# A decoder trunk on one core: the scan norm's squares in a tile of their own, three weight splits behind the last layer norm of a stage, and the small operations of the final norm first

## The chip, the cores and the metric

The kernel runs on one core of a Trainium2 chip. A core has a matrix engine (TensorE, "PE" in the profile, with its weight loads shown apart as "PEld"), a vector engine (VectorE, "DVE"), a scalar engine (ScalarE, "ACT"), GpSimd ("POOL") and SyncE ("SP"), which here issues the transfers between DRAM and the on-chip memory. Each engine works through its own instructions in a fixed order and waits on semaphores for what the others make. The metric is the device time of one execution in microseconds. Before the change three runs took 1351.21, 1352.62 and 1352.86 us, so the median is 1352.62 us.

## The reference

The reference is a two-layer decoder trunk on a residual stream of 512 tokens by 1024 columns, in float32:

1. A Mamba-2 (SSD) mixer: an input projection, a causal depthwise convolution of width 4 with SiLU, a chunked scan over 8 groups of 4 heads, a gate, a root-mean-square norm inside each group, and an output projection.
2. `h = layer_norm(alpha * h + mix)`.
3. A gated feed-forward network (FFN) with a causal depthwise convolution of width 3: `(silu(g) * val) @ down`, hidden size 2816, and again `h = layer_norm(alpha * h + ff)`.
4. A latent-attention layer (8 heads) with a layer norm, and a second FFN with the final layer norm, whose result is the output.

The group norm of step 1 is the place of the first part of the change:

```
yg = y.reshape(b, s, G, SSD_D_INNER // G)
yg = yg * lax.rsqrt(jnp.mean(yg * yg, axis=-1, keepdims=True) + LN_EPS)
```

## The kernel before, in words

**Products.** Every float32 product is made of three passes on TensorE. A weight tile is split into a rounded part `wh` (a cast on ScalarE, line 60) and a rest `wl` (a subtraction on VectorE, line 61); activations are split in the same way into index 0 and index 1 of a tile. `mm_a` (line 117, matmuls at line 124) adds `wh` times the rounded activations, `wl` times the rounded ones and `wh` times their rest; `mm_b` (lines 130 to 132) does the same with the operands' roles turned round.

**The weight stream.** `WStream` holds the list of all weight tiles of the four stages in the order of use. A tile is loaded by SP into one of 3 staging buffers (`wst`, line 47), then split into one of 6 pairs of `wh` and `wl`. `ahead(i, la)` splits up to item `i + la`, but never more than 6 beyond the last retired one; `get` calls it with the default of 4. A staging buffer comes free when line 61 has read it, so a late split makes a later load late; a pair comes free when TensorE has used it.

**Order.** Python emits the instructions, and a planner then orders those of PE, DVE, ACT and POOL with its own costs; SP's transfers keep the order in which the program emits them (a load is emitted when a split makes room in the staging buffers). A tile in a pool of one buffer gets its next writer only after the last reader of the old contents is done, and the planner puts that writer where it expects this to be.

**The scan.** For each group `g`, `chain(g)` has seven steps. Step s2 (line 551) multiplies the decay matrix W (line 560) and makes `xdt` (line 565) and `wx` (line 567) from transposed inputs in PSUM. Step s3 multiplies `wx` on TensorE (line 574), then W and `xdt` (line 585). Step s4 ends with the sum of squares `sq` (line 608), which lies in the buffer of `wx` (`tag="wx"`). Step s5 reads `sq` on TensorE (line 614), s6 makes the group's factor `rstd`. For groups 0 to 6 the program has s5 of the group before ahead of s2; for the last group, 7, s5 of group 6 comes after s2 of group 7, just ahead of s3. Output projections (`out_part`, lines 130 to 132, and the addition to `h` on VectorE, line 150) fill the time between.

**From the scan to the first FFN.** The last `out_part` of each of four token blocks is followed by `ln_apply`: a sum on DVE (line 157), the squares on ACT (line 159), the power -0.5 on POOL (lines 160 and 161), and the normalisation on DVE (lines 164 and 167). `transpose_h` then transposes the block on TensorE (line 208), and ACT and DVE split the transposes into `ht` (lines 211 and 212). The transposes of the last two blocks are kept in `k.pend`. The FFN starts with its first four weight tiles, here called n to n+3, on tokens 0 to 255, flushes `k.pend` ahead of the fourth, and then does the four again on tokens 256 to 511 (lines 276 to 281). The weights n to n+2 are split before; n+3 to n+5 are split as the FFN asks for them.

**The final norm.** `ln_last` (line 169) normalises the last token block in two pieces of columns as TensorE ends them: statistics of the first 768 columns (lines 181 to 185), then of the last 256 (lines 186 to 191), the power on POOL (line 192), and the two normalising operations over the columns with the output transfers (lines 194 to 198).

## Time and profile before

| what | value |
|---|---|
| median of three runs | 1352.62 us |
| the profiled execution, its own time | 1353.32 us |
| span of that execution in the profile | 1351.6 us |
| mean granted clock of TensorE over the span | 0.995 |
| busy share of PE, PEld, DVE, ACT, POOL | 99%, 83%, 65%, 43%, 5% |
| moved by the DMA engines | 135.14 MB, 100 GB/s on the mean |

Times inside the profile count from the start of the span. A row of the timeline gives start, length, engine, line and operation, with "xN" where several were merged; in square brackets stands how long the engine had been idle before it and what released it. A row of the windows view gives the length of a stretch, then the busy time of PE, PEld, DVE, ACT and POOL with their instruction counts in brackets, the TensorE clock that was granted on the mean (1.00 is full speed), the busy share of the DMA engines and GB/s. Matmuls are pipelined, so the distance of their starts tells more than their length.

### The profile page before, as it was taken

The page shows a single profiled execution, that of the slowest core. Times are in us where ns is not written, and L with a number is a line of the kernel's source. Part 1 is how long each engine was busy: PE and PEld are TensorE (multiplying, and loading weights), DVE is VectorE, ACT ScalarE, POOL GpSimd, SP SyncE. Part 2 cuts the span into 40 slices and gives each one's busy share as a digit, 9 for nine tenths or more (in the row PEclk, how much of TensorE's full clock was granted, in tenths as well). Part 3 has the DMA queues.
Part 4 walks back from the last instruction along what each step waited for, and adds up shares of the span by engine and source line. Part 5 has one row for each costly group of instructions (what it writes and reads, how often), then busy time and mean ns, then how long its engine had stood idle before and what let it go on. Part 6 is the DMA issues. An engine that isn't in the chain of part 4 may idle for free.

```text
span 1351.6 us, 17208 instructions
## 1 busy us (share of the span) xinstructions
PE 1335.6 (99%) x6827; PEld 1126.3 (83%) x6827; DVE 879.8 (65%) x1326; ACT 586.3 (43%) x934; POOL 70.8 (5%) x71
## 2 busy tenths in 40 slices
PE   9999999999999999999999999999999999999997
PEld 8888888888878888888888889888898888888886
DVE  7788888778788655525655366987576553465534
ACT  5765546545533444313443134665254432344421
POOL 0111001101102000000000021000100000000001
PEclk9999999999999999999999999999999999999999
DMA  7533332332322333232332222211052322323211
GB/s 241 185 101 122 110 119 69 110 125 79 109 94 64 142 99 103 87 102 94 102 101 86 86 89 65 86 54 64 32 190 94 98 98 89 106 95 103 91 55 63
DMA packets 44433, 135.14 MB, mean 100 GB/s; under 512 B 4768, under 2 KB 5792, under 8 KB 42816
## 3 DMA queue, kind: packets, MB, share of 16 engines
q1 hardware_dynamic: 44352, 134.04, 30.1%
q8 instruction: 53, 0.87, 0.3%
q14 instruction: 28, 0.23, 0.1%
HBM read 131.86 MB, written 2.16 MB: 99 GB/s over the span
## 4 chain that ended last, share of the span: by engine, by line
PE 90%; DVE 5%; issue 1%; DMA 1%; ACT 1%; POOL 1%; SPq 0%; POOLq 0%; DVEq 0%; ACTq 0%
PE ps L124 55%; PE ps L130 9%; PE ps L131 9%; PE ps L132 9%; PE ps L1039 2%; PE ps L585 1%; PE ps L1073 1%; PE ps L574 1%; DVE wl L61 1%; PE ps L593 1%; DVE h L150 1%; PE ps L1060 1%; PE ps L693 1%; PE ps L208 1%; PE ps L556 1%
## 5 line engine op out<-in xcount | busy, mean ns | idle before, releaser
L124 PE MATMUL ps<-ht,wh 128*128 128x512 f32 (+1 forms) x2272 | 519.5, 379 | 0.5 <-DVE ht L212 0.3
L124 PEld LDWEIGHTS ps<-ht,wh 128*128 128x128 f32 x2272 | 409.7, 189 | 79.7 <-issue 1.0
L61 DVE TENSOR_TENSOR wl<-wst,wh 128x1024 fp32r<-128x1024 f32 (+3 forms) x226 | 265.4, 1179 | 154.3 <-ACT wh L60 153.9
L60 ACT CAST wh<-wst 128x1024 fp32r<-128x1024 f32 (+3 forms) x226 | 228.1, 1014 | 229.0 <-PE ps L132 168.7
L124 PE MATMUL ps<-ht,wl 128*128 128x512 f32 (+1 forms) x1136 | 267.9, 378 | 0.0
L124 PEld LDWEIGHTS ps<-ht,wl 128*128 128x128 f32 x1136 | 206.5, 189 | 39.5
L130 PE MATMUL ps<-wh,gt 128*128 128x512 f32 (+1 forms) x363 | 139.1, 383 | 0.0
L132 PE MATMUL ps<-wh,gt 128*128 128x512 f32 (+1 forms) x363 | 138.9, 383 | 0.0
L131 PE MATMUL ps<-wl,gt 128*128 128x512 f32 (+1 forms) x363 | 138.9, 383 | 0.0
L243 DVE SCALAR_TENSOR_TENSOR acc<-ps,cw,acc 128x511 f32<-128x511 f32 x88 | 65.5, 746 | 97.1 <-ACT acc L242 97.1
L446 DVE SCALAR_TENSOR_TENSOR cv<-ps,cw,cv 128x511 f32<-128x511 f32 (+2 forms) x96 | 71.4, 745 | 37.9 <-ACT cv L444 37.2
L242 ACT ACTIVATE acc<-ps,cw 128x512 f32<-128x512 f32 x88 | 68.5, 779 | 40.3 <-PE ps L124 40.3
L132 PEld LDWEIGHTS ps<-wh,gt 128*128 128x128 f32 x363 | 68.2, 188 | 13.3
L131 PEld LDWEIGHTS ps<-wl,gt 128*128 128x128 f32 x363 | 68.2, 188 | 13.3
L130 PEld LDWEIGHTS ps<-wh,gt 128*128 128x128 f32 x363 | 68.2, 188 | 13.2
L249 ACT CAST gt<-acc 128x512 fp32r<-128x512 f32 x44 | 27.3, 621 | 98.6 <-DVE acc L248 98.6
L244 DVE SCALAR_TENSOR_TENSOR acc<-ps,cw,acc 128x510 f32<-128x510 f32 x88 | 65.6, 748 | 2.8
L150 DVE SCALAR_TENSOR_TENSOR h<-h,ps 128x512 f32<-128x512 f32 x47 | 31.2, 683 | 55.0 <-PE ps L132 55.0
L247 ACT ACTIVATE acc<-acc 128x512 f32<-128x512 f32 x44 | 27.8, 632 | 86.9 <-DVE acc L244 86.9
L160 POOL TENSOR_SCALAR lnst<-lnst 128x1 f32<-128x1 f32 x15 | 11.6, 772 | 867.9 <-ACT lnjunk L159 867.9
L548 ACT ACTIVATE W<-W,cum 128x128 f32<-128x128 f32 x128 | 41.0, 392 | 26.7 <-DMA W<-cumd 26.7
L130 PE MATMUL ps<-wh,yT 128*128 128x512 f32 x128 | 50.8, 397 | 0.0
(229 smaller groups left out, 1548.8 us busy)
## 6 DMA issues: line engine op xcount, KB each, us to landing
wst<-in_up_dram SPq DMA_DIRECT2D x88, 512.0 KB, 3.4
wst<-in_down_dram SPq DMA_DIRECT2D x40, 512.0 KB, 3.5
wst<-in_xbc_dram SPq DMA_DIRECT2D x32, 512.0 KB, 3.9
W<-cumd SPq DMA_DIRECT2D x8, 1024.0 KB, 4.7
wst<-in_sow_dram SPq DMA_DIRECT2D x16, 512.0 KB, 3.7
wst<-in_zw_dram SPq DMA_DIRECT2D x14, 512.0 KB, 3.5
lngb<-in_gb_dram SPq DMA_DIRECT2D x4, 1024.0 KB, 6.2
wst<-in_aow_dram SPq DMA_DIRECT2D x8, 512.0 KB, 3.4
```

Of the source, the lines that this page charges most:

```text
L60: nc.scalar.copy(h[:, :f], s[:, :f])
L61: nc.vector.tensor_tensor(l[:, :f], s[:, :f], h[:, :f], op=ALU.subtract)
L124: nc.tensor.matmul(out, w[:, k, :], xts[k][:, x, ts], start=first and p == 0 and k == 0, stop=last and p == 2 and k == nk - 1, skip_group_ ...
L130: nc.tensor.matmul(out, xt[:, 0, tsl], wh, start=start, stop=False, skip_group_check=True)
L131: nc.tensor.matmul(out, xt[:, 0, tsl], wl, start=False, stop=False, skip_group_check=True)
L132: nc.tensor.matmul(out, xt[:, 1, tsl], wh, start=False, stop=stop, skip_group_check=True)
L150: self.nc.vector.scalar_tensor_tensor(hs, a, scale, b, op0=ALU.mult, op1=ALU.add, **kw)
L242: nc.scalar.activation(a, b, AF.Identity, bias=cw[:, ch, 3:4], scale=cw[:, ch, 2:3])
L243: nc.vector.scalar_tensor_tensor(a[:, 1:], b[:, :SEQ - 1], cw[:, ch, 1:2], a[:, 1:], op0=ALU.mult, op1=ALU.add)
L244: nc.vector.scalar_tensor_tensor(a[:, 2:], b[:, :SEQ - 2], cw[:, ch, 0:1], a[:, 2:], op0=ALU.mult, op1=ALU.add)
L446: nc.vector.scalar_tensor_tensor(t[:, d:], b[:, :SEQ - d], cw[:, ch, 3 - d:4 - d], t[:, d:], op0=ALU.mult, op1=ALU.add)
L548: nc.scalar.activation(w, w, AF.Relu, bias=D["cum"][:, c, g * HPG + h:g * HPG + h + 1], scale=-1.0)
```

## The change

The change has four edits. (1) `sq` gets a buffer of its own, and the small tiles `warm` and `ropet` share one. (2) In an FFN that starts with pending transposes, the splits of n+3 to n+5 are emitted behind the flush and tied behind `k.ln_end`, the last instruction of the last `ln_apply`, on DVE. Look-ahead arguments are made smaller so that they are not emitted sooner, in `out_part` too. (3) In `ln_last` the mean shift `d` is begun from the first 768 columns while ACT works, the remaining small operations are put in another order, and (4) the two large operations with `nmu` are tied behind the last small one, `v`.

```
-        self.warm = self.const.tile([P, P], F32, name="warm")
+        self.warm = self.const.tile([P, P], F32, name="warm", tag="ropet")
...
-            nc.vector.scalar_tensor_tensor(hv[:, sl], hv[:, sl], rstd, self.gb[:, 1, sl], op0=ALU.mult, op1=ALU.add)
+            self.ln_end = nc.vector.scalar_tensor_tensor(hv[:, sl], hv[:, sl], rstd, self.gb[:, 1, sl], op0=ALU.mult, op1=ALU.add)
...
+        nc.vector.tensor_scalar(d, sa, -1.0 / DM, c, op0=ALU.mult, op1=ALU.subtract)
         nc.vector.tensor_scalar(q, qa, 1.0 / DM, LN_EPS, op0=ALU.mult, op1=ALU.add)
         nc.vector.scalar_tensor_tensor(h3, h3, 1.0, bs[1], op0=ALU.mult, op1=ALU.add, accum_out=sb)
-        nc.vector.tensor_scalar(nmu, sb, sa, -1.0 / DM, op0=ALU.add, op1=ALU.mult)
         nc.scalar.activation(junk[:, 768:], h3, AF.Square, bias=c, accum_out=qb)
-        nc.vector.tensor_scalar(d, nmu, c, None, op0=ALU.subtract)
+
+        nc.vector.tensor_scalar(d, sb, -1.0 / DM, d, op0=ALU.mult, op1=ALU.add)
         nc.vector.tensor_scalar(e, d, d, q, op0=ALU.mult, op1=ALU.subtract)
-        nc.vector.tensor_scalar(v, qb, 1.0 / DM, e, op0=ALU.mult, op1=ALU.subtract)
+        nc.vector.tensor_scalar(nmu, d, c, None, op0=ALU.add)
+        last = nc.vector.tensor_scalar(v, qb, 1.0 / DM, e, op0=ALU.mult, op1=ALU.subtract)
         nc.gpsimd.tensor_tensor(rstd, v, self.mhalf, op=ALU.pow)
...
+        with self.tc.issue_after(last.ins):
+            for sl in (slice(0, 512), slice(512, 1024)):
+                nc.vector.scalar_tensor_tensor(hv[:, sl], hv[:, sl], nmu, self.gb[:, 0, sl], op0=ALU.add, op1=ALU.mult)
+        for sl in (slice(0, 512), slice(512, 768), slice(768, 1024)):
+            nc.vector.scalar_tensor_tensor(hv[:, sl], hv[:, sl], rstd, self.gb[:, 1, sl], op0=ALU.mult, op1=ALU.add)
+            nc.sync.dma_start(out[:, sl], hv[:, sl])
...
+                for i in range(3):
+                    k.mm_a(bs[i][:, :256], wv(i, 2 - i), k.ht, slice(0, 256))
+                k.flush()
+                with tc.issue_after(k.ln_end.ins):
+                    ws.ahead(n + 3, 0)
+                    ws.ahead(n + 5, 0)
+                k.mm_a(bs[3][:, :256], wv(3, 0), k.ht, slice(0, 256))
                 for i in range(4):
-                    if i == 3:
-                        k.flush()
-                    k.mm_a(bs[i][:, :256], wv(i, 3 - i), k.ht, slice(0, 256))
-                for i in range(4):
-                    k.mm_a(bs[i][:, 256:], wv(i), k.ht, slice(256, 512))
+                    k.mm_a(bs[i][:, 256:], wv(i, 0), k.ht, slice(256, 512))
...
-                S["sq"] = one.tile([P, SEQ], F32, name="sq", tag="wx")
+                S["sq"] = one.tile([P, SEQ], F32, name="sq")
...
-            w = [ws.get(n[0] + OFF[g] + j) for j in range(2)]
+            w = [ws.get(n[0] + OFF[g] + j, 4 - j) for j in range(2)]
...
-    t = c.tile([P, 2, N], F32, name="ropet")
+    t = c.tile([P, 2, N], F32, name="ropet", tag="ropet")
```

The planner's order of the instructions moves with it. The instructions of PE, ACT and POOL keep their order everywhere. On DVE it moves at three places that matter below, and on SP at one. In the changed kernel, lines of the FFN stand 2 further down and those of the scan 5 further down (line 567 is 572, line 212 is 214); lines 61, 150, 157, 164 and 167 keep their numbers.

The first place is VectorE at the last group's step s2. Before:

```order
L560 TENSOR_TENSOR W<-W,cbm 128x2048
L61 TENSOR_TENSOR wl<-wst,wh 128x1024
L565 TENSOR_TENSOR xdt<-ps,dt 128x512 x2
L150 SCALAR_TENSOR_TENSOR h<-ps,rstd,h 128x512 x6
L567 TENSOR_TENSOR wx<-ps,wend 128x512
L567 TENSOR_TENSOR wx<-ps,wend 128x256
L61 TENSOR_TENSOR wl<-wst,wh 128x1024
```

The same place in the changed kernel:

```order
L565 TENSOR_TENSOR W<-W,cbm 128x2048
L570 TENSOR_TENSOR xdt<-ps,dt 128x512
L572 TENSOR_TENSOR wx<-ps,wend 128x512
L570 TENSOR_TENSOR xdt<-ps,dt 128x512
L572 TENSOR_TENSOR wx<-ps,wend 128x256
L150 SCALAR_TENSOR_TENSOR h<-ps,rstd,h 128x512 x6
L61 TENSOR_TENSOR wl<-wst,wh 128x1024 x2
```

`wx` now stands ahead of the six additions to `h` and of a split that stood ahead of it. In groups 3 to 6 one split moves behind two or three additions of line 150, and all of these stay ahead of `wx`.

The second place is VectorE from the third block's normalisation to the first convolution of the FFN. Before:

```order
L212 TENSOR_TENSOR ht<-ps,ht 128x4x128 x2
L61 TENSOR_TENSOR wl<-wst,wh 128x1024
L150 SCALAR_TENSOR_TENSOR h,lnst<-ps,rstd,h 128x512 x2
L61 TENSOR_TENSOR wl<-wst,wh 128x1024
L157 TENSOR_SCALAR lnst<-lnst 128x1
L61 TENSOR_TENSOR wl<-wst,wh 128x1024
L164 SCALAR_TENSOR_TENSOR h<-h,lnst,lngb 128x512 x2
L167 SCALAR_TENSOR_TENSOR h<-h,lnst,lngb 128x512 x2
L212 TENSOR_TENSOR ht<-ps,ht 128x4x128 x4
L61 TENSOR_TENSOR wl<-wst,wh 128x1024
```

The same place in the changed kernel:

```order
L214 TENSOR_TENSOR ht<-ps,ht 128x4x128 x2
L150 SCALAR_TENSOR_TENSOR h,lnst<-ps,rstd,h 128x512 x2
L157 TENSOR_SCALAR lnst<-lnst 128x1
L164 SCALAR_TENSOR_TENSOR h<-h,lnst,lngb 128x512 x2
L167 SCALAR_TENSOR_TENSOR h<-h,lnst,lngb 128x512 x2
L61 TENSOR_TENSOR wl<-wst,wh 128x1024
L214 TENSOR_TENSOR ht<-ps,ht 128x4x128 x4
L61 TENSOR_TENSOR wl<-wst,wh 128x1024 x3
```

The three splits (n+3, n+4, n+5) leave the chain of the fourth block's norm: n+3 now comes right behind it, n+4 and n+5 behind the four rests of `ht`. On SP the FFN's `cw` and `lngb` transfers now stand ahead of the load of weight n+6 instead of behind it. At the start of the second FFN the order is as it was.

The third place is VectorE in the final norm. Before:

```order
L186 SCALAR_TENSOR_TENSOR h,lnlast<-h,ps 128x256
L187 TENSOR_SCALAR lnlast<-lnlast 128x1
L189 TENSOR_SCALAR lnst<-lnlast 128x1
L194 SCALAR_TENSOR_TENSOR h<-h,lnlast,lngb 128x512
L190 TENSOR_SCALAR lnst<-lnst 128x1
L194 SCALAR_TENSOR_TENSOR h<-h,lnlast,lngb 128x512
L191 TENSOR_SCALAR lnst<-lnlast,lnst 128x1
L197 SCALAR_TENSOR_TENSOR h<-h,lnst,lngb 128x512
```

The same place in the changed kernel:

```order
L187 SCALAR_TENSOR_TENSOR h,lnlast<-h,ps 128x256
L190 TENSOR_SCALAR lnst<-lnlast,lnst 128x1
L191 TENSOR_SCALAR lnst<-lnst 128x1
L192 TENSOR_SCALAR lnlast<-lnst,lnlast 128x1
L193 TENSOR_SCALAR lnst<-lnlast,lnst 128x1
L197 SCALAR_TENSOR_TENSOR h<-h,lnlast,lngb 128x512 x2
L199 SCALAR_TENSOR_TENSOR h<-h,lnst,lngb 128x512
```

The last small operation (line 191 before, 193 now), on which POOL's power waits, now stands ahead of both large operations with `nmu`.

6 lines of the change are left out of this document (removed).

## The prediction

> **What bounds the kernel now.** I read the busy times first, then who waited for whom on TensorE, then the windows and timelines around the two longest waits.
>
> ```profile
> PE 1335.6 (99%) x6827; PEld 1126.3 (83%) x6827; DVE 879.8 (65%) x1326; ACT 586.3 (43%) x934; POOL 70.8 (5%) x71
> ...
> PE ps L574 <- DVE wx L567: 2.5, 1, 2.5
> PE ps L208 <- DVE h L167: 2.0, 1, 2.0
> ...
> PE ps L124 <- DVE ht L212: 0.3, 1, 0.3
> ```
>
> PE is the bound almost everywhere, so only what shortens PE's own line of work, or the tail behind its last matmul, can move the time. Its waits are few. The two longest, 2.5 and 2.0 us, each happen once, and the first two edits touch just these two instructions. The windows show that each wait costs more than itself:
>
> ```profile
> 343.13:346.32 3.19, 3.19 (x39) 2.58 (x38) 2.31 (x4) 1.99 (x3) 0.00 (x0) 1.00 0.29 119
> 383.36:385.95 2.59, 0.06 (x4) 0.00 (x0) 2.59 (x5) 1.22 (x3) 0.00 (x0) 1.00 0.02 6
> 385.95:390.96 5.01, 5.01 (x38) 4.09 (x38) 4.14 (x7) 0.37 (x1) 0.00 (x0) 0.66 0.39 119
> ...
> 438.81:440.79 1.98, 0.00 (x0) 0.03 (x1) 1.54 (x3) 0.67 (x2) 0.97 (x2) 1.00 0.19 46
> 440.79:445.29 4.50, 4.50 (x25) 4.32 (x25) 2.91 (x5) 1.17 (x2) 0.00 (x0) 0.62 0.67 244
> ```
>
> The first row is lines 574 and 585 of group 6 at full clock: 3.19 us. In group 7 the same work follows an empty 2.59 us and takes 5.01 us at a granted clock of 0.66. The second wait is followed by 4.50 us at 0.62. Both times the clock drops soon after the gap.
>
> **Edit 1, sq out of the buffer of wx.** VectorE and TensorE at the last group:
>
> ```profile
> 376.73 2.29 DVE L560 TENSOR_TENSOR W<-W,cbm 128x2048 f32<-128x2048 f32 x1
> 378.93 1.22 DVE L61 TENSOR_TENSOR wl<-wst,wh 128x1024 fp32r<-128x1024 f32 x1
> 380.07 1.28 DVE L565 TENSOR_TENSOR xdt<-ps,dt 128x512 f32<-128x512 f32 x2
> 381.27 4.03 DVE L150 SCALAR_TENSOR_TENSOR h<-ps,rstd,h 128x512 f32<-128x512 f32 x6
> 385.22 1.01 DVE L567 TENSOR_TENSOR wx<-ps,wend 128x512 f32<-128x512 f32 x2
> ...
> 383.00 0.43 PE L614 MATMUL ps<-sq,ones 128*32 128x128 f32 x8
> 385.95 1.92 PE L574 MATMUL ps<-wx,bk 128*128 128x256 f32 x6 [2.53 <-DVE wx L567]
> ```
>
> Before, wx could not be written until line 614 had read sq at 383.4, and it stood behind six additions that end at 385.2. Now xdt and wx follow W directly: from 378.9 they take 1.28 + 1.01 = 2.3 us and end at 381.2, 2.2 us before PE is through with line 614. The split that was ahead of them (1.13 us from its start to the next) goes behind the six additions, and these start where they started, at 381.2 instead of 381.27. The PSUM banks that lines 574 and 585 need come free with the first three additions, at some 0.67 us each by 383.3, or with wx itself; the additions from the fourth to the sixth end by 385.2, before PE writes the next projections. The wait of 2.53 goes, and with it the slow stretch, 5.01 - 3.19 = 1.82. **Edit 1: -4.35 us.** Bounds: -2.5 if the clock dropped all the same, -4.5 with the first slowed matmul behind it.
>
> What is behind: the split goes from 380.1 to about 386.4, and with it one load on SP. Two later splits ended at 387.3 and 389.0 anyway, so the third staging buffer comes free when it did before. PE first uses the FFN's weights some 40 us later. The splits moved behind two or three additions in groups 3 to 6 stand ahead of the same wx as before, and PE never waited there. I cost both at nothing; without that cover each would cost the 1.13 us of a split. That warm and ropet share a buffer costs nothing either: the one is read by the first matmuls of the program, the other written in the middle of the FFN.
>
> **Edit 2, splits behind the norm.** VectorE, ScalarE and TensorE at the fourth block's norm:
>
> ```profile
> 432.87 1.21 DVE L61 TENSOR_TENSOR wl<-wst,wh 128x1024 fp32r<-128x1024 f32 x1
> 434.00 0.73 DVE L150 SCALAR_TENSOR_TENSOR h<-ps,rstd,h 128x512 f32<-128x512 f32 x1
> ...
> 435.34 1.21 DVE L61 TENSOR_TENSOR wl<-wst,wh 128x1024 fp32r<-128x1024 f32 x1
> 436.48 0.20 DVE L157 TENSOR_SCALAR lnst<-lnst 128x1 f32<-128x1 f32 x1
> 436.60 1.21 DVE L61 TENSOR_TENSOR wl<-wst,wh 128x1024 fp32r<-128x1024 f32 x1
> ...
> 439.90 1.41 DVE L167 SCALAR_TENSOR_TENSOR h<-h,lnst,lngb 128x512 f32<-128x512 f32 x2 [0.44 <-POOL lnst L161]
> ...
> 433.34 1.05 ACT L60 CAST wh<-wst 128x1024 fp32r<-128x1024 f32 x1 [3.45 <-DMA wst<-in_up_dram]
> 436.77 1.15 ACT L159 ACTIVATE lnjunk<-h,lnst 128x1024 bf16<-128x1024 f32 x1 [2.38 <-DVE lnst L157]
> ...
> 436.81 1.12 PE L124 MATMUL ps<-ht,wh 128*128 128x256 f32 x8
> 437.77 1.04 PE L208 MATMUL ps<-ident,h 128*128 128x128 f32 x8
> 440.79 1.48 PE L208 MATMUL ps<-ident,h 128*128 128x128 f32 x8 [1.98 <-DVE h L167]
> 441.92 2.06 PE L124 MATMUL ps<-ht,wh 128*128 128x256 f32 x8
> ```
>
> Two of the three splits stand in the chain that ends in line 167: 434.00 - 432.87 = 1.13 and 436.48 - 435.34 = 1.14. The third, from 436.60 to 437.8, ends before ACT's Square does (436.77 + 1.15 = 437.9) and costs nothing. So line 167 starts at 439.90 - 2.27 = 437.63. PE followed it by 0.89; the second transposes could start at 438.5, and PE has ended the first eight at 438.7 to 438.8. The wait goes, with some 0.2 us to spare; the second half of h is ready at 439.0, just as PE comes to it. The eight transposes then take 0.9 to 1.0, so line 124 starts near 439.65 instead of 441.92: 2.3 us. Its first 16 matmuls took 445.29 - 441.92 = 3.37; at full clock 8 start in 437.77 - 436.81 = 0.96, so 16 take 1.92: another 1.45. **Edit 2: -3.75 us.** Bounds: -2.0 (clock still drops and a wait of 0.3 like that of line 212 comes back), -3.9.
>
> Late now: weight n+3's rest, split from 439.0 to 440.2. PE wants it after eight matmuls, at 439.65 + 0.96 = 440.6. It just fits; a miss would be some tenths. The rests of ht (line 212) come one split later, ending by 442.8, and are wanted after 24 + 16 matmuls, at 444.4. Weights n+4 and n+5 are split by 445.1 and wanted only when four quarters of 24 matmuls (2.88 each, from 442.5) are through, at 454. The cast of n+6 on ACT waits for a pair that PE frees with the first of these quarters, near 445.4, and now also for a load that lands up to 1 us after that (the slower rival below). Behind it on ACT stands the first convolution (line 242), and for that nobody waits soon: PE writes other banks until the convolution is long done.
>
> The second FFN starts in its old order, so it gives nothing. Everything behind depends on PE, which shows no other long wait, so both gains carry through to the end.
>
> **Edits 3 and 4, the final norm.** PE has ended:
>
> ```profile
> 1344.33 0.21 DVE L187 TENSOR_SCALAR lnlast<-lnlast 128x1 f32<-128x1 f32 x1
> ...
> 1344.70 0.74 DVE L194 SCALAR_TENSOR_TENSOR h<-h,lnlast,lngb 128x512 f32<-128x512 f32 x1
> ...
> 1346.21 0.21 DVE L191 TENSOR_SCALAR lnst<-lnlast,lnst 128x1 f32<-128x1 f32 x1
> 1347.07 1.54 DVE L197 SCALAR_TENSOR_TENSOR h<-h,lnst,lngb 128x512 f32<-128x512 f32 x3 [0.66 <-POOL lnst L192]
> ...
> 1344.74 0.19 ACT L188 ACTIVATION_READ_ACCUMULATOR lnjunk<-h,lnlast 128x1 f32 x1
> ```
>
> Before, v (line 191) started at 1346.21, though ACT's sum was there at 1344.93. Now d, e and nmu follow the addition as line 187 did, 0.12 to 0.25 apart, and v starts when ACT's sum is there, at about 1345.0. The two operations of 0.74 then take 1.41, like the pair of line 167 above, from 1345.15 to 1346.55, and under them POOL's power, which took 1347.07 - 1346.21 = 0.86 from v to line 197, is ready at 1345.9. Line 197 starts near 1346.5 instead of 1347.07: **-0.55 us**, between -0.35 (one more small operation of 0.21 in the way) and -0.65. The added first d runs while DVE waits for ACT.
>
> **Sum.** -4.35 - 3.75 - 0.55 = -8.65. The profiled execution took 1353.32 (span 1351.6): 1344.7, span 1343.0. It lay 0.7 above the median of 1352.62, so I expect a median of **1344.0**.
>
> [...]
>
> **Rivals.** *The clock drops at the transposes all the same.* After edit 2 PE runs 16 transposes of line 208 with nothing between.
>
> ```profile
> 437.77:441.64 3.87, 1.89 (x17) 1.50 (x16) 3.19 (x6) 1.50 (x5) 1.68 (x2) 1.00 0.10 23
> 41.36:45.09 3.73, 3.73 (x32) 3.36 (x31) 2.81 (x6) 3.69 (x7) 0.00 (x0) 1.00 0.52 147
> ```
>
> The first row is the stretch before the second drop: 1.89 us of transposes and a gap. It can't tell which of them counted. Against: the second row, 3.73 us of transposes and small matmuls in the scan's first group, kept the clock at 1.00, and the transposes now fill only 1.9 us. Edit 2 would then be worth 2.3: 1345.5. [...] 12%.
>
> *A late load takes the norm's place.* The cast at 433.34 waited 3.45 us for its load and stands ahead of the Square on ACT. It ends at 434.4; the Square will be due at 436.77 - 2.27 = 434.5. If the load lands 1 us later, line 167 and PE wait for 0.8 of it, and the clock may drop (1.45): 1344.8 to 1346.3; I take 1346. 12%.
>
> *The change doesn't do it for wx.* Something else holds lines 574 or 585, a bank or W. Then only edits 2 to 4 count: -4.3, 1348.3. The timeline shows W done at 379.0, so 4%.
>
> *Slower: weights run out in the first FFN.*
>
> ```profile
> wst<-in_up_dram SPq DMA_DIRECT2D x88, 512.0 KB, 3.4
> lngb<-in_gb_dram SPq DMA_DIRECT2D x4, 1024.0 KB, 6.2
> ...
> 45.09 16.34 PE ps L124 x72
> ```
>
> The three staging buffers are held until 440.2, 443.9 and 445.1, and the load of n+6 now comes behind lngb. A full weight lasts PE 16.34 / 3 = 5.45, so n+6 is wanted at 454 + 2 x 5.45 = 464.9. It should land by 440.2 + 6.2 = 446.4 and be split 2.3 later: 16 us to spare. From 16 us of lateness PE waits, and from 16 + 8.65 = 24.7 on the kernel is slower than before; at 28 us it takes 1356. Nothing in the rows is near that. 4%.
>
> **The numbers.** Forecast 66%, rivals 12, 12, 4 and 4, unnamed 2. A change under 0.2% (2.7 us) can't be told from none. All but the last two groups are faster by more: 0.92, with 0.03 for the same and 0.05 for slower. The forecast's own range is 1343.0 to 1345.0; to leave out no more than two in ten, with the clock rival, the late load and a run's spread of 0.8, I take 1342.7 to 1347.3.
>
> **What would show it.** Right: no wait of line 574's successor (579) for wx; a clock of 1.00 in the 5 us behind it; lines 579 and 590 in 3.2 us; no wait of the transposes above 0.3 us and no drop behind them; the first operation with rstd some 2.8 us behind the last matmul instead of 3.3; a span near 1343. Wrong: a clock under 0.8 behind the 16 transposes; the Square behind a late cast; PE waiting for wl (line 61) near 440 or 465; or the clock falling at another place.

## The result and the profile after

| | before | changed |
|---|---|---|
| median of the executions | 1352.89 us (6) | 1345.13 us (6) |
| lowest to highest | 1351.21 to 1354.15 | 1344.48 to 1347.20 |
| the profiled execution, its own time and span | 1353.32, 1351.6 | 1346.10, 1344.4 |
| mean granted clock in that profile | 0.995 | 0.998 |

The ratio of changed to before is 0.9945, with a 95% interval of 0.9933 to 0.9958: 5.7 to 9.1 us less. Line 574 is now 579, line 585 is 590 and line 208 is 210.

The first line of the page of the changed kernel on busy times, and its longest waits of TensorE:

```profile
PE 1332.5 (99%) x6827; PEld 1123.7 (84%) x6827; DVE 879.8 (65%) x1327; ACT 586.1 (44%) x934; POOL 71.1 (5%) x71
```

```profile
PE ps L698 <- ACT wh L60: 1.3, 1, 1.3
PE ps L415 <- DVE warm L100: 1.1, 1, 1.1
PE ps L132 <- DVE cT L969: 0.6, 1, 0.6
...
PE ps L124 <- DVE ht L214: 0.3, 1, 0.3
```

Both waits that headed the list before, 2.5 for wx and 2.0 for h, are gone. The first two rows belong to the first 10 us of the program and stood there before (0.8 and 1.1). The third is new.

The changed kernel's windows at the two places:

```profile
384.00:389.00 5.00, 5.00 (x46) 4.09 (x46) 5.00 (x7) 1.34 (x3) 0.00 (x0) 1.00 0.22 56
...
436.00:440.50 4.50, 4.50 (x40) 4.50 (x40) 4.50 (x7) 0.73 (x2) 0.00 (x0) 1.00 0.90 314
```

TensorE has no hole and no slow stretch. The timeline of the changed kernel, VectorE and TensorE:

```profile
379.98 0.68 DVE L572 TENSOR_TENSOR wx<-ps,wend 128x512 f32<-128x512 f32 x1
...
381.17 0.42 DVE L572 TENSOR_TENSOR wx<-ps,wend 128x256 f32<-128x256 f32 x1
381.50 4.03 DVE L150 SCALAR_TENSOR_TENSOR h<-ps,rstd,h 128x512 f32<-128x512 f32 x6
...
383.44 0.43 PE L619 MATMUL ps<-sq,ones 128*32 128x128 f32 x8
383.80 1.56 PE L579 MATMUL ps<-wx,bk 128*128 128x256 f32 x6
385.29 1.97 PE L590 MATMUL ps<-W,xdt 128*64 128x128 f32 x32
387.19 0.50 PE L130 MATMUL ps<-wh,yT 128*128 128x512 f32 x1
...
433.98 1.41 DVE L167 SCALAR_TENSOR_TENSOR h<-h,lnst,lngb 128x512 f32<-128x512 f32 x2 [0.43 <-POOL lnst L161]
...
434.00 2.10 PE L210 MATMUL ps<-ident,h 128*128 128x128 f32 x16
435.86 1.20 PE L124 MATMUL ps<-ht,wh 128*128 128x256 f32 x8
...
1337.02 0.28 PE L132 MATMUL ps<-wh,gt 128*128 128x256 f32 x1
...
1339.88 1.54 DVE L199 SCALAR_TENSOR_TENSOR h<-h,lnst,lngb 128x512 f32<-128x512 f32 x3
```

wx is done at 381.6, and line 579 follows line 619 with nothing between. The 16 transposes run in one piece. From the end of the last matmul (1337.02 + 0.28 = 1337.30) to the first operation with rstd it is 2.58 us, against 3.25 before.

**Where the 7.2 us of span came from.** Both kernels have 6827 matmuls in the same order, so the start of each can be compared, counted from the first one. By this comparison, on the clock of before, the changed kernel's lead grows by 4.19 us from 384.9 to 389.3 us (edit 1) and by 3.58 from 439.7 to 443.7 (edit 2); the tail behind the last matmul gives 0.67 (edits 3 and 4). That makes 8.44. It loses 0.4 at the first weights, and from 838 to 853 us, in the latent attention (MLA), another 0.9. The latter begins with a load of in_vw, whose row in the view of DMA issues reads (median us to landing last), before and changed:

```profile
wst<-in_vw_dram SPq DMA_DIRECT2D x1, 512.0 KB, 4.9
```

```profile
wst<-in_vw_dram SPq DMA_DIRECT2D x1, 512.0 KB, 5.9
```

It was issued at the same place and landed 1.0 us later; the cast behind it on ScalarE, what stands behind that, and then line 132 waited 0.6 us for cT.

### The profile page after: what moved, and what is told of

The parts are those of the page before. It is cut to its first block, busy times and chain, and to the rows that moved or that the text cites. A ratio compares the mean times of both kernels' runs of the same rounds, so it can differ in the third digit from the quotient of the medians.

```text
span 1344.4 us, 17208 instructions
## 1 busy us (share of the span) xinstructions
PE 1332.5 (99%) x6827; PEld 1123.7 (84%) x6827; DVE 879.8 (65%) x1327; ACT 586.1 (44%) x934; POOL 71.1 (5%) x71
## 4 chain that ended last, share of the span: by engine, by line
PE 93%; DVE 3%; DMA 1%; ACT 1%; POOL 1%; issue 1%; SPq 0%; DVEq 0%; ACTq 0%; POOLq 0%
PE ps L124 56%; PE ps L130 9%; PE ps L131 9%; PE ps L132 9%; PE ps L1044 2%; PE ps L590 1%; PE ps L1078 1%; PE ps L598 1%; PE ps L579 1%; PE ps L1065 1%; DVE wl L61 1%; PE ps L210 1%; PE ps L561 1%; PE ps L698 1%; PE ps L536 1%
```

## The experiments

### Each part alone

The kernel before with one part of the change each.

```
# edit 1 alone
...
-                S["sq"] = one.tile([P, SEQ], F32, name="sq", tag="wx")
+                S["sq"] = one.tile([P, SEQ], F32, name="sq")
```

> Edit 1 alone: sq in a buffer of its own, and warm and ropet share one; the splits and the final norm are as before. Theory (a wait and a slow stretch that it causes): the wait of 2.53 us of line 574 for wx goes, the 5 us behind it run at a granted clock of 1.00, and TensorE is 4.2 us ahead from there on, as it was in the changed kernel at this place (384.9 to 389.3 us). The wait of 2.0 us of line 208 for h and the drop to 0.62 behind it stay. Time near 1348.5, against 1352.9. Rival (the two stretches are not independent: with the first drop gone the second goes too, or gets longer): the 4.5 us behind line 208's wait show another clock than 0.62, and the gain is 5.6 or more, or 2.8 or less. Rival (the 0.9 us that the changed kernel lost in MLA come of edit 1 alone): the lead shrinks to 3.3 us near 840 to 850 us, where an operation of line 132 then waits for cT; without that the lead of 4.2 stays to the end.

```
# edit 2 alone
...
+                k.flush()
+                with tc.issue_after(k.ln_end.ins):
+                    ws.ahead(n + 3, 0)
+                    ws.ahead(n + 5, 0)
...
-            w = [ws.get(n[0] + OFF[g] + j) for j in range(2)]
+            w = [ws.get(n[0] + OFF[g] + j, 4 - j) for j in range(2)]
```

> Edit 2 alone: the three splits behind the last layer norm. sq still shares wx's buffer. Theory: the wait of 2.53 us of line 574 and the drop to 0.66 behind it stay; the wait of line 210 for h is under 0.3 us, the 4.5 us behind it run at 1.00, and TensorE is 3.6 us ahead behind the place. Time near 1349.3. Rival (the clock drops because of the 16 transposes, and it did not in the changed kernel only because the first drop had gone): the stretch behind shows 0.6 to 0.8, and the lead is 2.1 us, a time near 1350.8. On the loss in MLA: if it comes with the moved splits and the look-ahead of the weights, TensorE loses 0.9 us near 840 to 850 us here too, and the time is near 1350.2; if it is a load that lands late by chance, it comes here, or not, without regard to the edit.

```
# edits 3 and 4 alone: the new ln_last
...
+        with self.tc.issue_after(last.ins):
+            for sl in (slice(0, 512), slice(512, 1024)):
+                nc.vector.scalar_tensor_tensor(hv[:, sl], hv[:, sl], nmu, self.gb[:, 0, sl], op0=ALU.add, op1=ALU.mult)
```

> Edits 3 and 4 alone: the final norm with its small operations first. Theory: from the last matmul's end to the first operation with rstd 2.6 us instead of 3.25, nothing else changes: 0.65 us less, a time near 1352.2, which lies within a measurement's spread. Rival (the gain is given back, since the two additions of nmu now both stand ahead of the first piece that is written out, and the first output transfer starts later): the span is within 0.2 us of before, with the last transfer landing at the same distance behind the last matmul. Both waits of 2.5 and 2.0 us stay.

| | median (executions) | ratio to before, 95% | difference of medians |
|---|---|---|---|
| before, beside these three and the next | 1352.29 (30) | | |
| edit 1 alone | 1348.41 (10) | 0.9962 to 0.9981 | -3.9 |
| edit 2 alone | 1349.14 (9) | 0.9967 to 0.9989 | -3.2 |
| edits 3 and 4 alone | 1352.53 (10) | 0.9993 to 1.0012 | +0.2 |

Edit 1 alone did what was expected: no wait, a clock of 1.00 behind it, a lead of 4.2 us behind the place, which grew by 0.4 in MLA (the in_vw load landed in 4.3 us). Edit 2 alone kept the clock at 1.00 behind the transposes, but one wait was left. Waits, then ScalarE and TensorE of the timeline, of edit 2 alone:

```profile
PE ps L208 <- DVE h L167: 0.7, 1, 0.7
```

```profile
434.16 1.05 ACT L60 CAST wh<-wst 128x1024 fp32r<-128x1024 f32 x1 [4.59 <-DMA wst<-in_up_dram]
435.11 1.14 ACT L159 ACTIVATE lnjunk<-h,lnst 128x1024 bf16<-128x1024 f32 x1
...
439.13 1.23 PE L208 MATMUL ps<-ident,h 128*128 128x128 f32 x8 [0.65 <-DVE h L167]
```

The cast waited for its load, the Square stood behind it, and TensorE waited 0.65: the prediction's late load, without a drop of the clock.

Edits 3 and 4 alone shortened the tail from 3.25 to 2.58 us as expected (the last matmul ended at 1342.33, the first operation with rstd started at 1344.91), but in times they can't be told from nothing. The profiles tell them apart: from the end of the last matmul to the end of the span it is 7.75 to 7.77 us in the five profiled kernels with the old final norm (before, edit 1 alone, edit 2 alone, and the runs below with the gap filled and with the old final norm) and 7.08 to 7.18 in the eight with the new one. So the 0.67 is there, and the rival by which the output transfers take it back falls. The surprise of this run is at the wx gap, which it did not touch. Its waits, and the windows of three equal stretches of 3.41 us:

```profile
PE ps L576 <- DVE wx L569: 2.5, 1, 2.5
```

```profile
380.86:384.27 3.41, 2.27 (x17) 1.41 (x15) 3.41 (x7) 2.14 (x3) 0.00 (x0) 1.00 0.49 155
384.27:387.68 3.41, 2.03 (x16) 1.59 (x18) 3.25 (x7) 0.39 (x2) 0.00 (x0) 1.00 0.00 0
387.68:391.09 3.41, 3.41 (x37) 2.90 (x32) 2.57 (x5) 0.00 (x0) 0.00 (x0) 1.00 0.67 193
```

The same wait of 2.5 us, and no drop behind it. The kernel before, in stretches laid the same way:

```profile
383.61:387.02 3.41, 1.07 (x5) 0.97 (x6) 3.41 (x6) 0.97 (x2) 0.00 (x0) 1.00 0.00 0
387.02:390.43 3.41, 3.41 (x29) 2.76 (x29) 3.07 (x6) 0.37 (x1) 0.00 (x0) 0.50 0.48 156
```

The trace keeps the moments at which the granted clock changes. Their distances, from the first change to full speed on:

```
us at           full     half   full    half   full
before         382.293  3.413  51.200  3.413  901.119
edit 1 alone   430.079  3.413 901.119
edit 2 alone   382.293  3.413 955.732
edits 3+4      433.493  3.413 904.532
```

All are whole multiples of 3.413 us (112, 1, 15, 1 and 264 of them in the first row). So in these profiles the granted clock changed only at whole steps of 3.413 us. In the run above the gap was cut by the edge of a step into 1.14 and 1.38 us of standing still; before, 2.34 us of it lay in one step, and the next step ran at half clock. The first change to full speed came 4.0 to 7.2 us into the span (5.4 and 6.2 in the two profiles of the changed kernel), so the steps lay differently to the program from one execution to the next. The lead also shows what the drop at this place cost: without it, the run with edits 3 and 4 alone gained 1.62 us on before, close to the half of 3.413.

### The gap filled

Fifteen matmuls that nobody needs in front of line 574, in the kernel before.

```
                 for c in range(NT):
                     nc.tensor.matmul(b[32 * c:32 * c + 32, :P], ones[:, :32], S["sq"][...], start=True, stop=True)
+                if g == NG - 2:
+                    yf = S["yT"][0]
+                    for _ in range(15):
+                        nc.tensor.matmul(b[:, P:], yf[:, 0, :P], yf[:, 0, P:], start=True, stop=True, skip_group_check=True)
```

> The kernel before, but in the last group 15 matmuls that nobody needs (384 columns each, about 0.165 us each, 2.5 us in all) stand between line 614 and line 574, where TensorE waits 2.53 us for wx. They fill the gap; wx comes no earlier. This takes the wait's own price and the clock's apart. Theory (the empty gap makes the clock drop): the first matmul of line 574 still starts at about 385.9 us, or 0.1 to 0.3 later; the clock stays at 1.00 behind it, lines 574 and 585 take 3.2 us instead of 5.01, and the time is 1.5 to 1.8 us less, near 1351.2. The wait for h and its drop stay. Rival (the clock drops for another reason, as the small matmuls of 64 rows or the reads of a just-written wx, or with a period of its own): lines 574 and 585 still run at 0.66 in 5 us, and the time is the same as before, 1352.9, or some tenths more.

Measured: 1351.87 (10 executions), ratio 0.9982 to 1.0001, 0.4 us less. TensorE in the timeline, then the windows of the steps at the norm, where this run's gap was left as it was:

```profile
383.80 2.88 PE L618 MATMUL ps<-yT 128*128 128x384 f32 x15
386.52 1.46 PE L574 MATMUL ps<-wx,bk 128*128 128x256 f32 x6
387.90 1.97 PE L585 MATMUL ps<-W,xdt 128*64 128x128 f32 x32
389.80 0.50 PE L130 MATMUL ps<-wh,yT 128*128 128x512 f32 x1
...
439.63 1.23 PE L208 MATMUL ps<-ident,h 128*128 128x128 f32 x8 [1.99 <-DVE h L167]
```

```profile
435.34:438.75 3.41, 2.30 (x20) 2.06 (x19) 2.73 (x6) 2.32 (x4) 1.68 (x2) 1.00 0.26 89
438.75:442.17 3.42, 2.54 (x21) 2.39 (x22) 3.42 (x6) 1.17 (x2) 0.00 (x0) 1.00 0.31 74
442.17:445.58 3.41, 3.41 (x30) 3.41 (x30) 0.37 (x1) 0.00 (x0) 0.00 (x0) 1.00 1.00 407
```

With the gap filled, lines 574 and 585 took 3.28 us to the next matmul (386.52 to 389.80) at full clock instead of 5.01, though line 574 now started 0.57 later than before. That fits the theory that the standing still slows them, but one profile can't show it, since the run above had the gap and no drop; the runs with made gaps below show it. The gain is 0.4 and not 1.5 to 1.8; if before does not pay the drop in every execution, that is what is to be expected (worked out below). And the gap of 1.99 us at the norm, cut into 1.11 and 0.88, cost no clock here.

### A theory of steps, and a kernel full of gaps

The new theory, from the clock records above: a step of 3.413 us in which TensorE stands still long enough is followed by one at half clock, which costs 1.71 us (an estimate, the half of 3.413; the run above gave 1.62); the steps run on by themselves, so how a gap lies to them is chance. To find the limit, 40 gaps were made in the FFNs of the changed kernel.

```
+    def gap(self):
+        w = 768 + 128 * (self.gaps % 8)
+        self.gaps += 1
+        b = self.bank()
+        x = self.small.tile([P, 64], F32, name="gapx")
+        for c in range(4):
+            self.nc.tensor.matmul(b[:, c * P:(c + 1) * P], self.ident, self.ident, start=True, stop=True)
+        for a in range(0, w, 512):
+            e = min(512, w - a)
+            self.nc.scalar.mul(b[:, :e], b[:, :e], 1.0)
+        self.nc.scalar.copy(x, b[:, :64])
+        self.last = self.nc.tensor.matmul(b[:, :64], self.ident, x, start=True, stop=True)
...
-                    k.mm_a(b, w, k.ht, slice(0, 512))
+                    with tc.issue_after(k.last.ins) if k.last else ExitStack():
+                        k.mm_a(b, w, k.ht, slice(0, 512))
```

> The changed kernel with 40 gaps made on purpose, one behind each pair of up-projections in both FFNs: TensorE does four small matmuls, ScalarE works on their bank for 0.8 to 2.3 us, and TensorE has nothing to do until a last small matmul may read what ScalarE left. Extra work only. The gaps should be some 1.2 to 2.8 us long, longer where a cast stands ahead on ScalarE. What counts is which of them is followed by a half clock. Theory of windows: exactly those steps of 3.413 us in which TensorE stood still for more than 1.9 us (1.87 was not followed by one so far, 1.98 was) are followed by one step at half clock; gaps of one length drop the clock or not by how they lie to the steps: those below 1.9 us never, those of 2.0 to 2.6 us in a share of (3.41 + gap - 2 x 1.9) / 3.41, which is 0.47 at 2.0 and 0.65 at 2.6. So 5 to 20 drops. Rival (the gap's own length decides, as the prediction's working had it): every gap above some length drops it, none below, with no overlap of the lengths. Rival (something of the two places of before made the drops, not the gaps): no drop at all.

It was executed once, as were the next two kernels. Its waits, and the windows of two gaps of one length, 2.15 us, step by step:

```profile
PE ps L229 <- ACT gapx L228: 91.8, 36, 3.2
```

```profile
474.78:478.19 3.41, 3.11 (x18) 2.55 (x16) 0.92 (x2) 1.78 (x3) 0.00 (x0) 1.00 0.47 154
478.19:481.61 3.42, 1.57 (x8) 1.36 (x9) 2.89 (x4) 2.19 (x5) 0.00 (x0) 1.00 0.03 10
481.61:485.02 3.41, 3.41 (x10) 2.64 (x9) 0.69 (x1) 0.16 (x1) 0.00 (x0) 0.50 0.39 144
...
1365.66:1369.07 3.41, 2.97 (x18) 2.43 (x16) 0.91 (x2) 1.92 (x3) 0.00 (x0) 1.00 0.54 151
1369.07:1372.48 3.41, 1.70 (x8) 1.46 (x9) 2.75 (x4) 2.18 (x5) 0.00 (x0) 1.00 0.18 18
1372.48:1375.90 3.42, 3.42 (x16) 2.82 (x15) 0.69 (x1) 0.03 (x1) 0.00 (x0) 1.00 0.41 143
```

In the first, 1.85 us of the gap lay in one step and the next ran at half clock; in the second 1.71, and it did not. All steps of this run up to its last matmul in which TensorE stood still for more than 0.6 us, put in order:

```
us idle in the step     0.70 ... 1.48  1.58  1.61  1.71 | 1.81  1.85  1.92  1.95 ... 3.08
clock of the next step  1.00 ... 1.00  1.00  1.00  1.00 | 0.50  0.50  0.50  0.50 ... 0.50
steps                              25                   |              25
```

Not one stands on the wrong side. By this reckoning the limit in this run lies between 1.71 and 1.81 us, about half a step. Behind each gap stand two small matmuls of 64 columns (0.24 us); if they count as standing still too, as the next run suggests, the limit would be 1.95 to 2.05, an estimate from these 0.24 us. Of the 36 gaps (four more were filled with other matmuls), which took 2.04 to 3.16 us, 25 were followed by a drop; among gaps of 2.04 to 2.76 us there are both outcomes, a gap of 2.04 that dropped and one of 2.76 that did not. The rival by which a gap's own length decides falls. The gaps came out longer than planned, and by the first reckoning my limit of 1.9 was a little high, which is why there are more drops than the 5 to 20 expected: for gaps of their lengths and a limit of 1.76, the share (3.41 + gap - 2 x 1.76) / 3.41, summed over the 36, is 25.8, an estimate beside the 25 measured.

### Gaps in pairs

```
+        for _ in range(2):
+            x = self.small.tile([P, 64], F32, name="gapx")
+            self.nc.scalar.mul(b[:, :w], b[:, :w], 1.0)
+            self.nc.scalar.copy(x, b[:, :64])
+            for c in range(4):
+                self.last = self.nc.tensor.matmul(b[:, c * 64:c * 64 + 64], self.ident, x, start=True, stop=True)
```

> As the run with 40 gaps, but each is broken in two by four small matmuls: two gaps of some 0.9 to 1.4 us, 0.3 to 0.9 us apart. None is as long as the shortest gap that was followed by a drop so far. Theory of windows (the sum of TensorE's idle time in a step counts, wherever it lies): where both gaps lie in one step and add up to more than 1.9 us, a half-clock step follows, and nowhere else. Rival (the step looks for one idle stretch without a break): no drop at all, though sums reach 2.0 to 2.6 us.

Windows of this run, a step and the next:

```profile
1417.50:1420.90 3.40, 2.18 (x17) 2.04 (x18) 2.72 (x4) 1.61 (x5) 0.00 (x0) 1.00 0.21 33
1420.90:1424.30 3.40, 3.40 (x10) 2.64 (x10) 0.19 (x1) 0.00 (x0) 0.00 (x0) 0.50 0.30 122
```

The gaps were 0.7 to 1.6 us each. Here TensorE stood still for 3.40 - 2.18 = 1.22 us in all (1.26 from the matmuls one by one), no stretch longer than 0.75, and the clock dropped. The limit by this sum was lower than expected: of the steps at full clock, those with up to 1.18 us idle had no drop, from 1.26 on each had one. Between the halves of a gap stand matmuls of 64 columns, which the profile counts as 1.1 us of work. The steps at half clock suggest that the granted clock did not go by this count. Two in a row:

```profile
1400.40:1403.80 3.40, 3.40 (x12) 3.02 (x13) 0.69 (x1) 0.53 (x1) 0.00 (x0) 0.50 0.54 161
1403.80:1407.20 3.40, 3.40 (x9) 2.64 (x8) 0.00 (x0) 0.00 (x0) 0.00 (x0) 0.50 0.00 0
```

In the first of them TensorE was never idle, but 1.5 us of it were matmuls of 64 columns, and the clock stayed at half for another step. So it was with 17 of the 53 steps at half clock: idle time alone was 0.66 us at most, but idle time and small matmuls together came to 1.52 us or more; in the other 36 they came to 1.38 at most. So the rival does not fall: if the small matmuls count for little, the two gaps and what stands between them are one long stretch. Whether gaps with ordinary matmuls between them add up was not tested.

### Transposes four times over

```
-    def transpose_h(self, i):
+    def transpose_h(self, i, times=1):
...
-                nc.tensor.transpose(b[:, j * P:(j + 1) * P], self.h[:, i, k * P:(k + 1) * P], self.ident)
+                for _ in range(times):
+                    nc.tensor.transpose(b[:, j * P:(j + 1) * P], self.h[:, i, k * P:(k + 1) * P], self.ident)
```

> The changed kernel, but each of the 16 transposes that are flushed behind the scan's last layer norm is done four times: 64 transposes, some 7.4 us in a row with no other matmul, so that at least one whole step of 3.413 us holds nothing else, however the steps lie. Theory (transposes count as work): the clock stays at 1.00 in and behind them, and the time is 5.6 us (48 x 0.116) above the changed kernel's, less what a late norm would have cost anyway: near 1350.6. Rival (transposes don't count as work; the 16 of the changed kernel were too short to show it): at least one step at half clock, which shows as transposes at 0.23 us each or as the matmuls behind them at 0.24 us instead of 0.12, and 1.7 us or more on top: 1352.4 or more.

Measured: 1350.79. TensorE, and the windows in and behind the transposes:

```profile
434.70 7.15 PE L211 MATMUL ps<-ident,h 128*128 128x128 f32 x64
```

```profile
434.70:441.60 6.90, 6.90 (x66) 6.90 (x65) 6.70 (x8) 1.76 (x3) 0.00 (x0) 1.00 0.56 195
441.60:445.50 3.90, 3.90 (x35) 3.90 (x34) 0.69 (x1) 0.59 (x1) 0.00 (x0) 1.00 0.85 331
```

One whole step, from 436.1 to 439.5 us, held nothing but transposes, and the clock stayed at 1.00. Unlike the gaps, they did not bring it down.

### The changed kernel again, and three variants

All four on one chip, with four executions each.

> The changed kernel, word for word, once more, as the yardstick for the three beside it. Theory of windows (from the clock records of the first six profiles: the clock is granted in steps of 3.413 us that run on by themselves; a step in which TensorE stood still for 1.98 us or more was followed by one at half clock, one with 1.64 us or less was not; so whether a gap of 2.0 to 2.6 us costs the 1.7 us depends on how it lies to the steps, which differs from execution to execution): the changed kernel has no gap above 1 us behind its start, so no drop in any execution; its times lie closer together than those of before (1349.0 to 1355.1, standard deviation 1.5), and the median is near 1345.1 again. On MLA: the load of in_vw took 5.9 us to land in the changed kernel's first profile and 4.2 to 5.3 in the five others; if that is chance, the wait of line 132 for cT (0.6 us) is not there in this one unless the load takes over 5.5 us; if the change brings it, it is there again.

```
# one split back: weight n+3 ahead of the norm again
+                ws.ahead(n + 3, 0)
                 with tc.issue_after(k.ln_end.ins):
-                    ws.ahead(n + 3, 0)
                     ws.ahead(n + 5, 0)
```

> The changed kernel, but one of the three splits (weight n+3) is queued ahead of the last layer norm again; the other two stay behind it. The norm comes 1.13 to 1.4 us later, and TensorE, which had no time to spare there (0.0 to 0.2 us), waits 0.9 to 1.3 us in front of the second eight transposes. Theory of windows: a gap of that size never fills a step of 3.413 us by 1.98 us, so the clock stays at 1.00 behind it in every execution, and the time is 0.9 to 1.3 us above the changed kernel's: near 1346.2. Rival (each gap of a microsecond is followed by a drop, as the prediction's working had it for the two gaps of before): 2.4 to 3.0 us above, near 1347.9, with a row at 0.6 to 0.7 behind the gap. Rival (it costs nothing, since another wait takes up the time): the same as the changed kernel.

```
# the old final norm: edits 3 and 4 undone
...
-        with self.tc.issue_after(last.ins):
-            for sl in (slice(0, 512), slice(512, 1024)):
-                nc.vector.scalar_tensor_tensor(hv[:, sl], hv[:, sl], nmu, self.gb[:, 0, sl], op0=ALU.add, op1=ALU.mult)
+        for sl, n in ((slice(0, 512), 1), (slice(512, 1024), 2)):
+            nc.vector.scalar_tensor_tensor(hv[:, sl], hv[:, sl], nmu, self.gb[:, 0, sl], op0=ALU.add, op1=ALU.mult)
...
```

> The changed kernel with the final norm of before: edits 3 and 4 undone, edits 1 and 2 kept. The edits alone could not be told from nothing against the times of before, which scatter by 1.5 us because of the clock; here both kernels of the comparison have no drop. Theory: the first operation with rstd starts 3.25 us behind the last matmul instead of 2.58, and the median is 0.65 us above the changed kernel's. Rival (the output transfers hide it): the same as the changed kernel, within 0.3 us, with the last landing at the same distance from the last matmul.

```
# the Square first
+        self.ln_sq = nc.scalar.activation(junk, hv, AF.Square, bias=nmu, accum_out=var)
...
-                with tc.issue_after(k.ln_end.ins):
+                with tc.issue_after(k.ln_end.ins), tc.issue_after(k.ln_sq.ins):
```

> The changed kernel, and on ScalarE the Square of the last layer norm is queued ahead of the casts of n+4 and n+5, which wait for loads (in the run of edit 2 alone such a load kept the cast until 434.2 us, the Square behind it came 1.1 us late, and TensorE waited 0.65 us for h; in the changed kernel's profile it was 0.1 us late and cost nothing). Theory (head of the line): the Square starts within 0.2 us of line 157's end whatever the load does; no wait of line 210 for h; in executions with a prompt load nothing changes, in those with a late one up to 1 us is saved: the median 0 to 0.4 us below the changed kernel's. Rival (the casts come too late now, as n+3's and n+4's weights are wanted by TensorE at 440 us): a wait of line 124 for wl or wh of up to 1 us, and a time above the changed kernel's.

| | median | lowest to highest | ratio to before (1352.06, 7 executions), 95% |
|---|---|---|---|
| changed | 1345.84 | 1343.92 to 1346.50 | 0.9936 to 0.9966 |
| one split back | 1345.35 | 1344.88 to 1346.89 | 0.9937 to 0.9966 |
| old final norm | 1346.39 | 1346.24 to 1346.62 | 0.9941 to 0.9974 |
| Square first | 1344.81 | 1344.06 to 1345.66 | 0.9931 to 0.9960 |

*Changed again*: no drop, as expected: its profile has none, and all four executions had a mean clock of 0.999, which leaves no room for one. That its times lie closer together is not shown by so few (standard deviation 1.1 us, against 1.3 of the seven of before beside it). The median is 6.2 us below before, by the interval 4.6 to 8.7, against 7.8 in the first comparison. The in_vw load took 5.6 us, and the wait for cT was 0.3. Over the profiles the lead over before that is gained or lost from 820 to 880 us goes with the time that this load takes:

```
in_vw landed after, us     4.1   4.3   4.5   4.9     5.3   5.6   5.9
lead gained from 820, us  +0.6  +0.4  +0.2  before  -0.5  -0.8  -1.0
```

The columns are the old final norm, edit 1 alone, edit 2 alone, before, edits 3 and 4 alone, changed again and changed. Two more at 4.3, one split back and the Square first, gained 0.4 and 0.5. Four kernels with the splits moved got the load in 4.1 to 4.5 us, so moving them does not by itself bring the late one. Both profiles of the changed kernel word for word had it late, 5.9 and 5.6; with two of them, chance is likely but not shown.

*One split back*: TensorE and the windows show the wait and a full clock behind it, as the theory of steps had it.

```profile
436.88 1.23 PE L210 MATMUL ps<-ident,h 128*128 128x128 f32 x8 [0.85 <-DVE h L167]
```

```profile
436.00:438.00 2.00, 1.15 (x10) 0.97 (x10) 2.00 (x4) 1.16 (x3) 0.00 (x0) 1.00 0.00 0
438.00:440.00 2.00, 2.00 (x19) 2.00 (x19) 2.00 (x4) 0.71 (x2) 0.00 (x0) 1.00 0.67 266
```

The 0.9 us were not seen in the medians: this one is 0.5 below the changed kernel's. With four executions that scatter by a microsecond that settles nothing, but the rival's 2.4 to 3.0 is hard to fit with it, and the clock of 1.00 behind the wait is against it. Matmul by matmul the cost is there: the lead gained from 391 to 800 us is 2.63, against 3.63 and 3.64 in the two profiles of the changed kernel, 1.0 less.

*Old final norm*: 0.55 us above the changed kernel, 3.25 us from the last matmul to rstd again; the expected 0.65 fits. Four executions alone would not show it; the distance from the last matmul to the end does (7.76 here). Here too a cast was kept by its load, until 430.90, and line 208 waited 0.5 us for h without a drop.

*Square first*: ScalarE and TensorE of its timeline:

```profile
430.27 1.15 ACT L159 ACTIVATE lnjunk<-h,lnst 128x1024 bf16<-128x1024 f32 x1 [6.64 <-DVE lnst L157]
431.42 2.93 ACT L60 CAST wh<-wst 128x1024 fp32r<-128x1024 f32 x3
...
427.51 1.21 PE L124 MATMUL ps<-ht,wh 128*128 128x256 f32 x8 [0.72 <-DVE ht L214]
```

The Square no longer waits for a load, and no weight came late; but the planner also moved an earlier split of transposes, and TensorE waited 0.72 us for that. The median is 1.0 below the changed kernel's, with ranges that overlap. Matmul by matmul the lead gained from 391 to 800 us is 3.64, as in the changed kernel (3.63 and 3.64); the profile's shorter time comes from the first weights and from in_vw. So nothing was gained at this place. The new order also issues that load later (428.65 instead of 425.35 us), and what it is worth in an execution where the changed kernel's load lands late stays open.

## Why the prediction was right, and where it was not

**What bounds the kernel, and edits 1 to 4 by the profile.** Right. Edit 1 was put at 4.35 and gave 4.19 between the two profiled executions; edit 2 at 3.75 and 3.58; edits 3 and 4 at 0.55 and 0.67, since rstd came 2.58 us behind the last matmul, not 2.8. Together 8.65 and 8.44. The splits that moved cost nothing, as reckoned; line 167 starts at 433.98, which with the lead of 3.77 by then is 437.75 on the old clock, against the 437.63 of the prediction.

**"Both times the clock drops soon after the gap."** True of that execution, and priced as if it were so in each: 1.82 + 1.45 = 3.27 us of the sum. The runs show it to be chance: the same wait of 2.5 us was not followed by a drop with edits 3 and 4 alone, nor the one of 1.99 us with the gap filled. By an estimate with the limit at 1.76, the middle of 1.71 and 1.81, a gap of 2.53 us costs the 1.71 in a share of (3.41 + 2.53 - 3.52) / 3.41 = 0.71 of executions, one of 1.98 in 0.55: 1.26 drops on the mean, 2.15 us. By a limit of 1.96, which fits as well if small matmuls count as standing still, the shares are 0.59 and 0.43, 1.02 drops and 1.74 us. The profiled execution had both, 3.41. The 30 executions of before beside the single parts, sorted by the clock that was granted on the mean:

```
mean clock       executions   median span
0.995 to 0.996       10         1351.9
0.997                14         1350.35
0.998 to 0.999        6         1348.6
```

One drop is 1.71 / 1350 = 0.0013 of the mean clock, and the rows lie 1.55 and 1.75 us apart, a drop's price each, so these are mostly executions with two drops, one and none. The sorting is rough: behind the last matmul the clock was at half for another 2.5 to 5.6 us in the profiles, which moves the mean too, and two profiles with exactly one drop (edit 2 alone, edits 3 and 4 alone) show 0.998. The changed kernel's executions all had 0.998 or 0.999. The shares also account for the parts alone: edit 1 should give 4.19 - 1.71 + 0.71 x 1.71 = 3.7 on the mean, and the mean time fell by 3.85; edit 2 3.58 - 1.71 + 0.55 x 1.71 = 2.8, and it fell by 3.3; the filled gap 0.71 x 1.71 - 0.57 = 0.6, and it fell by 0.65. With ten executions each, such a mean is good to 0.35 to 0.5 us, so this does not tell the two limits apart.

**"It lay 0.7 above the median of 1352.62, so I expect a median of 1344.0."** This is the step that failed. The profiled execution paid both drops, 1.3 us more than the mean by the shares above; that accounts for its place above the median, and just these drops the change takes away. Without them the changed kernel has nothing left of that 0.7 to give back: the sum's own 1344.7 was the forecast to keep. The measured median of 1345.13 is 1.1 from 1344.0 and 0.4 from 1344.7. That it comes so close is in part luck: the second measurement gave 1345.84.

**"Both gains carry through to the end."** Not in the profiled execution, where 0.9 went in MLA and 0.4 at the start; behind 880 us its lead no longer changes. Both losses hang on when a load lands, and both vary by as much in kernels with and without the change: the first weights (line 693 before, 698 after) kept TensorE 0 to 2.2 us in the profiles. Of the 0.4 between 1344.7 and the median this may be the cause; it was not tested.

**The rivals.** *The clock drops at the transposes all the same*: no, and 7.15 us of them, which the profile lists as MATMUL, did not do it either: the clock stayed at 1.00 in that run. *A late load takes the norm's place*: this happened. The chance put on it was too low and its price too high: of the six profiles with all three splits behind the norm and the transposes done once, two show TensorE waiting 0.65 and 0.5 us for h behind a late cast, and the gap was too short to touch the clock. *The change doesn't do it for wx* and *weights run out*: nothing of either in any run.

## What to carry to other kernels

Here a gap on TensorE cost about its own length (0.85 us of waiting and 1.0 us of lead with one split back), and, when more than about half a clock step of it lay in one step (1.81 us or more of 3.413 in the run with 40 gaps), also the part of a step that was lost at half clock, 1.62 us as measured at one place; how often was estimated from its length, and one profiled execution shows only one throw. So before a profiled execution's time is shifted to the median of others, ask which of its costs are chance, and whether the change takes just those away. A transfer that a cast waited for kept everything that stood behind that cast on its engine, and cost 0.5 and 0.65 us of TensorE's time in two profiles. Queuing the short operation of a critical chain ahead of the cast took this wait away, but look at what the planner moves in exchange: here TensorE waited 0.72 us for a split that it moved, and nothing was gained.

## What the runs showed of the hardware that I had not expected

- In these profiles the granted clock of TensorE changed only at whole steps of 3.413 us, counted through the whole program from the first full speed on. In the run with 40 gaps a step with 1.81 us or more of its time idle was followed by one at half clock and a step with 1.71 or less was not (50 steps without an exception). In the four records tabled above each step at half clock was followed by full clock. In the other profiles, that of the pairs left aside, no step before the last matmul contradicts this; in the old final norm's, a step with 1.87 us idle, which reaches beyond the last matmul, was followed by a full one. With small matmuls counted as idle the limit would be above 1.95 by the estimate above, and this step fits too; that was not tested.
- Pairs of gaps with eight matmuls of 64 columns between them were followed by half clock from 1.26 us of idle time in all, and in 17 steps at half clock with 0.66 us idle at most, but 1.52 us or more of idle time and such matmuls together, the clock stayed at half for another step. That such matmuls count for less than full work is my reading of it. With 7.15 us of transposes of 128 columns the clock stayed at 1.00.
- A transfer of 512 KB by the same instruction at the same place landed after 4.1 to 5.9 us, and with that the lead over before moved by -1.0 to +0.6 us.
- About half of the variance of the kernel before goes with the clock: its 30 executions beside the single parts spread from 1348.99 to 1355.12 (standard deviation 1.5), within the rows of the table above by 1.06 (1 - 1.06 x 1.06 / (1.5 x 1.5) = 0.5). The changed kernel's ten executions spread from 1343.92 to 1347.20 (1.0).
